# Queries by seven products, the ratio on GpSimd and rows in pairs, in a two-layer decoder trunk

## The chip, the cores and the metric

The kernel runs on one core of a Trainium2 chip. The metric is the device time in microseconds (us) of one execution; of several runs the median is taken. One more execution was recorded by the hardware profiler, and all views of the profile come from that one. The engines are called TensorE (PE in the profile, and PEld for its weight loads), VectorE (DVE), ScalarE (ACT), GpSimd (POOL) and SyncE (SP), whose queue issues most DMA transfers.

## The reference

The input `x` (512 rows of 1024) gets 16 learned meta rows ahead of it, 528 rows in all. Two layers follow, each with a norm, one input projection, a mixing step, a gate and an output projection of width 2048 to 1024; then a last norm. Layer 1 is gated linear attention and the change does not touch it. Layer 2 is differential attention with 8 heads; per head the two softmax maps are subtracted:

```python
q, k, v, z = jnp.split(xn @ w_in, 4, axis=-1)        # 2048 columns each, 256 a head
s = jnp.einsum('bhpqd,bhpkd->bhpqk', qb, kh) * scale + bias   # p = 0, 1: two maps of 128 columns
p = jax.nn.softmax(causal(s), axis=-1)
a = p[:, :, 0] - lam * p[:, :, 1]
o = head_rms(jnp.einsum('bhqk,bhkv->bhqv', a, vh)) * gnorm * (1.0 - lambda_init)
y = jax.nn.silu(z) * o
h = h + y @ w_out
```

Inputs and output are float32.

## The kernel before

**Numbers.** Every matmul operand in float32 is kept as two parts, a rounded `hi` and the rest `lo`; a product is the sum of `hi*hi`, `hi*lo` and `lo*hi`. The helper `split` (lines 276 to 280) makes the parts: ScalarE copies `hi`, VectorE subtracts to get `lo`. So each weight block that is used is passed once through ScalarE and once through VectorE.

**Two forms of a projection.** A block of 256 output columns of a projection (one head's queries, keys, values or gates) is made in one of two ways.
- *Plain* (`project`, matmul at line 421): for each 128 columns, 8 blocks of the contraction times three terms, each matmul 512 columns wide. The weights come in by `load_w` and are split as two pairs (`want_diff`).
- *A unit* (class `Unit`, `product` with the matmul at line 431): a 2 by 2 block scheme of the Strassen-Winograd kind, seven products instead of eight, each of 12 matmuls over half of the rows (256 columns without the meta rows, 264 with them). `want_unit` loads the weights and makes, on VectorE, four sums of 128x512 (line 366), and five operands: the single blocks `a11`, `a12`, `a22` and the pairs `s21` and `s43`. The products are `first` (p1) and `p2` to `p7`. p1, p6 and p7 accumulate in one PSUM bank, `self.bx`; after each of them `partial` (line 452) has ScalarE copy the bank to SBUF. `add` (lines 477 and 479) has VectorE combine another bank with such a copy. When half of the output is there, `tail` is called.

A unit knows whether the next thing in the queue is a unit too (`nxt`); then it computes that one's first product ahead of its own last two, and the next one finds itself `early`. A unit that is `early` and has no `nxt` is called lone here.

**Buffers.** PSUM has banks `bx` (two of them), `by`, `bv` (one each) for projections, and four `ps` for the attention. Weight operands have one buffer for each single block and two for pairs; raw weights have two.

**The order of the work.** TensorE's order is the order of the program text. A `Weaver` (`W`) holds a queue of generators, one a projection; `W.fill(us)` runs them for about so many microseconds by the costs that they yield, and between two fills the program issues a step of the attention. The other engines are ordered by the scheduler, by readiness and by priority (`urgent`, `at_once`, `soon` raise it). Each engine executes in its order.

**The head loop** (the loop over `hd` near the end of `trunk`). In pass `hd` the attention of head `hd` is woven with the projections for head `hd + 1`: first, in passes 2 to 6, `q_diff_out2`, an output projection of an earlier pair of heads (matmuls at line 400, and an add into `hacc` on VectorE at line 1783 for each row block); then gates `z`, values `v`, keys `k` as units and queries `q` plain. In pass 6 the order is `k`, `q`, `v`, `z`. The steps of the attention are, for each of four blocks of 128 query rows:
- `A` = `scores`: matmuls of `q` and `k` (line 400, `ps<-k,q`), for each of the two maps a VectorE instruction that adds the bias and finds the minimum (line 1692), an exponential on ScalarE with its row sum (1694); then on VectorE the reciprocal of the second map's sum (1697), the ratio `lam * sum0 / sum1` (1698), and the combination of both maps (1699).
- `B` = `turn`: transposes on TensorE, and their split.
- `C` = `values`: matmuls with `v`; ScalarE squares (1728), GpSimd takes the power -1/2 (1730), ScalarE scales (1731).
- `E` = `rows`: two transposes on TensorE (1737), a multiplication with the gate on VectorE (1740), and a split.

The first step `A(3)` of pass `hd` needs the queries that were the last projection of pass `hd - 1`. The last pass is cut short, and the rest of its steps is written out behind the loop, between the last output projections (line 1807).

## Time and profile before

| | |
|---|---|
| median of 3 runs | 971.12 us (970.82 to 972.05) |
| profiled execution | 970.65 us, of it 968.9 us from the first to the last instruction |
| ScalarE's copies of weight pairs (line 276, `wh<-raw`) | 98, 1054 ns each |
| VectorE's subtractions of weight pairs (line 277, `wl<-raw,wh`) | 98, 1221 ns each |
| ScalarE's copies of a unit's bank (line 452) | 120, 379 ns each |
| GpSimd's power in `values` (line 1730) | 32, 795 ns each |
| memory read and written | 83.64 and 11.80 MB, 99 GB/s over the span |

How to read the views: the page gives busy time and share of the span by engine, and the chain that ended last, followed back from the last instruction. A row of groups has line, engine, operation, output<-inputs, shapes and count; then busy us and mean ns of one; then the engine's idle time ahead of them and what ended most of it. A row of the timeline has the start in us, the duration in us, and the same names; in brackets the idle time before it. Matmuls overlap in the pipeline, so what one costs is read from start to start, not from its duration. A window's row gives the busy time of each engine in that stretch.

### The profile page before, as it was taken

The numbers are of one execution on the slowest core, as the hardware profiler recorded it, in microseconds if no ns is written. First come the engines' busy times: TensorE is split into PE (matmuls) and PEld (weight loads), VectorE is DVE, ScalarE is ACT, GpSimd is POOL, SyncE is SP. The second block draws the span as 40 slices with busy tenths as digits, with TensorE's granted clock in tenths as the row PEclk, the third lists the DMA queues.
The fourth block names the chain that finished last, engine by engine and source line by source line (L and its number), as shares of the span: only waits on it lengthen the run. The fifth ranks groups of instructions, "written<-read, shape, count | busy, mean of one in ns | idle before, by whom it ended". The sixth has DMA issues, their size and how long they took to land.

```text
span 968.9 us, 18048 instructions
## 1 busy us (share of the span) xinstructions
PE 957.2 (99%) x6993; PEld 906.9 (94%) x6993; DVE 778.6 (80%) x1586; ACT 626.8 (65%) x1304; POOL 44.9 (5%) x68
## 2 busy tenths in 40 slices
PE   9999999999999999999999999999999999999997
PEld 8999999999999999998899998998999989989996
DVE  7989885886888787668997987968869769687785
ACT  7776755577647567656757776575675756755583
POOL 1000000000000000000001001000000000000001
PEclk9999999999999999999999999999999999999999
DMA  7322223635363236124355525243342341722212
GB/s 197 88 85 59 82 79 122 147 103 128 116 162 91 85 117 158 53 101 152 99 130 138 143 73 133 75 139 98 99 138 88 118 119 44 182 70 84 89 64 87
DMA packets 128522, 104.94 MB, mean 108 GB/s; under 512 B 51102, under 2 KB 112830, under 8 KB 128433
## 3 DMA queue, kind: packets, MB, share of 16 engines
q1 hardware_dynamic: 123104, 93.80, 35.1%
q10 hardware_dynamic: 5328, 9.95, 2.8%
q8 instruction: 56, 0.92, 0.4%
q14 instruction: 34, 0.27, 0.1%
HBM read 83.64 MB, written 11.80 MB: 99 GB/s over the span
## 4 chain that ended last, share of the span: by engine, by line
PE 88%; ACT 1%; DVE 1%; issue 1%; POOLq 0%; DVEq 0%
PE bx L431 19%; PE bv L431 12%; PE by L431 10%; PE bx L421 10%; PE ps L400 9%; PE bx L972 5%; PE bx L400 3%; PE bv L972 2%; PE by L972 2%; PE ps L1214 2%; PE by L400 2%; PE bv L400 2%; PE ps L1807 1%; PE bx L1807 1%; PE bv L421 1%; PE by L421 1%
## 5 line engine op out<-in xcount | busy, mean ns | idle before, releaser
L277 DVE TENSOR_TENSOR wl<-raw,wh 128x1024 fp32r<-128x1024 f32 x98 | 119.4, 1221 | 23.0 <-ACT wh L276 18.9
L276 ACT ACTIVATE wh<-raw 128x1024 fp32r<-128x1024 f32 x98 | 103.1, 1054 | 48.3 <-PE by L972 22.9
L431 PE MATMUL bv<-x,wh 128*128 128x264 f32 (+1 forms) x656 | 98.6, 287 | 0.0
L431 PE MATMUL bx<-x,wh 128*128 128x264 f32 (+1 forms) x640 | 95.6, 286 | 0.0
L431 PEld LDWEIGHTS bv<-x,wh 128*128 128x128 f32 x656 | 86.8, 189 | 0.6 <-DVE z L479 0.2
L431 PEld LDWEIGHTS bx<-x,wh 128*128 128x128 f32 x640 | 84.6, 188 | 0.7 <-ACT u L452 0.2
L452 ACT ACTIVATE u<-bx 128x264 f32<-128x264 f32 (+1 forms) x120 | 45.3, 379 | 35.5 <-PE bx L431 33.1
L1694 ACT ACTIVATE p<-p,st 128x528 f32<-128x528 f32 (+3 forms) x64 | 36.5, 570 | 41.7 <-DVE st L1692 41.4
L421 PE MATMUL bx<-x,wh 128*128 128x512 f32 (+1 forms) x256 | 62.4, 385 | 0.0
L277 DVE TENSOR_TENSOR wl<-sum,wh 128x1024 fp32r<-128x1024 f32 x41 | 50.1, 1221 | 10.6 <-ACT wh L276 10.5
L431 PE MATMUL bx<-x,wl 128*128 128x264 f32 (+1 forms) x320 | 54.1, 284 | 0.0
L431 PE MATMUL bv<-x,wl 128*128 128x264 f32 (+1 forms) x328 | 53.8, 284 | 0.1
L421 PEld LDWEIGHTS bx<-x,wh 128*128 128x128 f32 x256 | 44.4, 188 | 7.8
L276 ACT ACTIVATE wh<-sum 128x1024 fp32r<-128x1024 f32 x41 | 43.1, 1051 | 9.7 <-PE by L972 3.9
L431 PE MATMUL by<-x,a12h 128*128 128x264 f32 (+1 forms) x320 | 47.5, 286 | 0.1
L1730 POOL TENSOR_TENSOR st<-st,mhalf 128x1 f32<-128x1 f32 x32 | 25.5, 795 | 468.6 <-ACT on L1728 418.2
L431 PE MATMUL bx<-x,a11h 128*128 128x264 f32 (+1 forms) x320 | 46.6, 284 | 0.0
L431 PEld LDWEIGHTS bv<-x,wl 128*128 128x128 f32 x328 | 45.4, 188 | 0.3 <-issue 0.3
L431 PEld LDWEIGHTS bx<-x,wl 128*128 128x128 f32 x320 | 45.3, 188 | 0.3
L431 PEld LDWEIGHTS bx<-x,a11h 128*128 128x128 f32 x320 | 42.4, 188 | 0.6
L431 PEld LDWEIGHTS by<-x,a12h 128*128 128x128 f32 x320 | 42.1, 188 | 0.3 <-ACT t L1658 0.3
L276 ACT ACTIVATE a11h<-raw 128x512 fp32r<-128x512 f32 x41 | 25.7, 626 | 20.7 <-DMA raw<-in_diff_w_in_dram 7.9
(493 smaller groups left out, 2631.9 us busy)
## 6 DMA issues: line engine op xcount, KB each, us to landing
raw<-in_gla_w_in_dram SPq DMA_DIRECT2D x48, 512.0 KB, 4.5
raw<-in_diff_w_in_dram SPq DMA_DIRECT2D x42, 512.0 KB, 4.9
raw<-in_diff_w_in_dram SPq DMA_DIRECT2D x11, 1024.0 KB, 5.9
raw<-in_gla_w_out_dram SPq DMA_DIRECT2D x8, 1024.0 KB, 5.8
raw<-in_diff_w_out_dram SPq DMA_DIRECT2D x8, 1024.0 KB, 6.0
vd<-planes ACTq DMA_DIRECT2D x12, 268.0 KB, 5.8
vd<-keep ACTq DMA_DIRECT2D x12, 264.0 KB, 2.3
T<-bdr SPq DMA_DIRECT2D x8, 264.0 KB, 4.7
```

The costliest lines, as they stand in the source:

```text
L276: act.activation(hi, src, AF.Copy)
L277: dve.tensor_tensor(lo, src, hi.bitcast(F32), op=ALU.subtract)
L400: pe.matmul(ps, l, r, start=first and n == 0, stop=last and n == 2, **kw)
L421: pe.matmul(bank, a[:, k, :], b[k] if n0 is None else b[k][:, n0 + i * nn:n0 + (i + 1) * nn], start=n == 0 and ks[0] == 0, stop=n == len(t ...
L431: pe.matmul(bank[:, :x[q].shape[2]], w[p][:, k * P:(k + 1) * P], x[q][:, k, :], start=first and i == 0, stop=i == len(PASSES) - 1, skip_gr ...
L452: W.moved = act.activation(t, self.bx[:, :self.n], AF.Copy, scale=self.sc)
L972: pe.matmul(banks[i][:, :HT], h.t[p][:, k, mm * P:(mm + 1) * P], s.y[q][k][:, i * HT:(i + 1) * HT], start=n == 0, stop=n == len(PASSES) - 1)
L1214: pe.matmul(o, s.kd[:, i, kc], s.qs[:, i, t0:t0 + n], start=i == 0, stop=i == 1)
L1694: act.activation(p[:, :nk], p[:, :nk], AF.Exp, scale=-1.0, bias=st[:, m:m + 1], accum_out=st[:, 2 + m:3 + m])
L1730: pool.tensor_tensor(ms, ms, mhalf[:, :1], op=ALU.pow)
L1807: pe.matmul(ps[i], yp[hd][p][:, k, b * P:(b + 1) * P], wt[q][cs.start // 512][:, 2 * hd + k, cs.start % 512:(cs.stop - 1) % 512 + 1], star ...
```

## The change

- Queries of heads 3 to 7 become units over the rows without meta; their tail splits the finished half into `s.q`.
- In layer 2 a lone unit computes p7 in a second `bx` bank of its own; VectorE adds the earlier copy to it instead of ScalarE copying the accumulated bank.
- `q_diff_out2`, behind the second part's row block 1 of its last half, issues the first product of the unit that follows it.
- In `scores` the second map is made before the first. The ratio moves from two VectorE instructions to three on GpSimd: a power of -1, and two multiplications.
- `rows` handles two blocks at once (except in the last head): four transposes, one multiplication and one split of twice the width. The loop has two `E` steps instead of four.
- The first fill of a pass is 4.0 instead of 3.0, and the least fills behind `B` and `E` are 2.4 and 1.0 instead of none.

```diff
@@ class Unit
+        @at_once
+        def third(self, bank):
+            t = T(up[0], [P, HT], F32, "u", bufs=3)[:, :self.n]
+            if self.sc == 1.0:
+                dve.tensor_tensor(t, bank[:, :self.n], self.u2, op=ALU.add)
+            else:
+                dve.scalar_tensor_tensor(t, bank[:, :self.n], self.sc, self.u2, op0=ALU.mult, op1=ALU.add)
+            return t
...
             def p7():
-                yield from product(self.bx, ws.use(s43)[1], X["t3"], False)
-                self.u3 = self.partial()
+                if W.second and early and not nxt:
+                    bank = pb_tile("bx")
+                    yield from product(bank, ws.use(s43)[1], X["t3"])
+                    self.u3 = self.third(bank)
+                else:
+                    yield from product(self.bx, ws.use(s43)[1], X["t3"], False)
+                    self.u3 = self.partial()
                 add(1, 1, self.bv, self.u3, -1)
@@ trunk
+    minus = cp.tile([P, 1], F32, name="minus")
+    dve.memset(minus, -1.0)
...
-    up[0] = ep
+    up[0], W.second = ep, True
@@ q_diff_q
+        scale, qts = -float(P) ** -0.5, []
+
+        def tiles():
+            assert not hd or heads[hd - 1].scored
+            s.q = [T(ep, [P, 2, NR], F32R, f"q{j}", bufs=1) for j in range(2)]
+
+        if hd in (3, 4, 5, 6, 7):
+            def dst():
+                tiles()
+                qts.extend([tok_tile()[:, :NR], tok_tile()[:, :NR]])
+                return qts
+
+            @soon
+            def tail(i):
+                split(*[t[:, i, :] for t in s.q], qts[i])
+
+            return W.add(Unit(want_unit(d_w_in, 256 * hd), Xr, scale, dst, tail), 8.9)
         want_diff(256 * hd)
@@ scores
-            r.p = []
+            r.p = [None, None]
...
-            for m in range(2):
+            for m in (1, 0):
...
-                r.p.append(p[:, :nk])
-
-            dve.reciprocal(st[:, 5:6], st[:, 3:4])
-            dve.scalar_tensor_tensor(st[:, 5:6], st[:, 5:6], lam, st[:, 2:3], op0=ALU.mult, op1=ALU.mult)
+                r.p[m] = p[:, :nk]
+
+            pool.tensor_tensor(st[:, 5:6], st[:, 3:4], minus, op=ALU.pow)
+            pool.tensor_tensor(st[:, 4:5], st[:, 2:3], lam, op=ALU.mult)
+            pool.tensor_tensor(st[:, 5:6], st[:, 5:6], st[:, 4:5], op=ALU.mult)
             dve.scalar_tensor_tensor(r.p[0], r.p[1], st[:, 5:6], r.p[0], op0=ALU.mult, op1=ALU.subtract)
@@ rows
-        def rows(r):
+        def rows(*rs):
+            w = P * len(rs)
             pt = ps_tile()
             for m in range(2):
-                pe.transpose(pt[:, m * P:(m + 1) * P], r.on[:, m * P:(m + 1) * P], ident)
-            y = T(ep, [P, 2, P], F32, "yt")
-            cs = slice(r.ta, r.ta + P)
-            W.mark = dve.tensor_tensor(y, pt[:, :256].rearrange("p (m c) -> p m c", m=2), s.z[:, :, cs], op=ALU.mult)
+                for j, r in enumerate(rs):
+                    pe.transpose(pt[:, m * w + j * P:m * w + (j + 1) * P], r.on[:, m * P:(m + 1) * P], ident)
+            y = T(ep, [P, 2, w], F32, "yt", bufs=1)
+            cs = slice(rs[0].ta, rs[0].ta + w)
+            W.mark = dve.tensor_tensor(y, pt[:, :2 * w].rearrange("p (m c) -> p m c", m=2), s.z[:, :, cs], op=ALU.mult)
...
-        return A, lambda b: turn(R[b]), lambda b: values(R[b]), lambda b: rows(R[b])
+        return A, lambda b: turn(R[b]), lambda b: values(R[b]), lambda b: rows(*([R[b]] if hd == D_HEADS - 1 else [R[b], R[b + 1]]))
@@ q_diff_out2
         def gen():
+            nxt = W.following()
+            nxt = nxt if isinstance(nxt, Unit) else None
...
                         yield 1.4
+                        if (i, j, b) == (halves[-1], 1, 1) and nxt:
+                            yield from nxt.first()
@@ head loop
-        steps = [(A, 0), (A, 1), (B, 0), (A, 2), (C, 0), (B, 1), (E, 0), (A, 3), (C, 1), (B, 2), (E, 1), (C, 2), (B, 3),
-                 (E, 2), (C, 3), (E, 3)]
+        steps = [(A, 0), (A, 1), (B, 0), (A, 2), (C, 0), (B, 1), (A, 3), (C, 1), (B, 2), (E, 1), (C, 2), (B, 3),
+                 (C, 3), (E, 3)]
...
-        W.fill(3.0)
+        W.fill(4.0)
...
-                       ((4.0, 3.0, 5.2, 3.0, 4.6, 3.0, 4.0, 3.0)[hd]) if n == len(steps) - 2 else 2.4 if f is C else 0.0))
+                       ((4.0, 3.0, 5.2, 3.0, 4.6, 3.0, 4.0, 3.0)[hd]) if n == len(steps) - 2 else {A: 0.0, B: 2.4, C: 2.4, E: 1.0}[f]))
```

More of the change, by code (lines that the diff above doesn't have):

```diff
@@ L78, in __init__ @@
         self.queue, self.late, self.left, self.stop = deque(), [], 0.0, None
-        self.away, self.behind, self.gated = [], [], ()
+        self.away, self.behind, self.gated, self.second = [], [], (), False
     def add(self, gen, us=0.0):
@@ L1668, in gen @@
                 yield from project(ws.take(), real2, None, NR, [by_halves(bank)])
-                assert not hd or heads[hd - 1].scored
                 if i == 0:
-                    s.q = [T(ep, [P, 2, NR], F32R, f"q{j}", bufs=1) for j in range(2)]
-                urgent(split)(*[t[:, i, :] for t in s.q], bank, scale=-float(P) ** -0.5)
+                    tiles()
+                urgent(split)(*[t[:, i, :] for t in s.q], bank, scale=scale)
         return W.add(gen(), 10.3)
```

## The prediction

> **What bounds the kernel now.** I read the page first: how full each engine is, and whose work the chain that ended last is made of.
>
> ```profile
> span 968.9 us, 18048 instructions
> PE 957.2 (99%) x6993; PEld 906.9 (94%) x6993; DVE 778.6 (80%) x1586; ACT 626.8 (65%) x1304; POOL 44.9 (5%) x68
> PE 88%; ACT 1%; DVE 1%; issue 1%; POOLq 0%; DVEq 0%
> ```
>
> TensorE is 99% busy, and 88% of the last chain is TensorE's own work. A busy TensorE can still hide waits, so I went on to the windows, one for each pass of the head loop that the change touches (a pass runs from one `A(3)` to the next), and two fuller stretches before them.
>
> ```profile
> core 0: us, PE busy (x) PEld busy (x) DVE busy (x) ACT busy (x) POOL busy (x), PEclk, DMA share, GB/s
> 460.00:520.00 60.00, 59.11 (x441) 56.44 (x441) 58.04 (x112) 39.05 (x79) 1.21 (x1) 1.00 0.44 113
> 485.00:548.00 63.00, 62.85 (x478) 60.36 (x476) 54.90 (x120) 41.42 (x98) 4.05 (x4) 1.00 0.58 141
> 667.87:730.90 63.03, 63.03 (x436) 58.70 (x434) 49.96 (x109) 41.14 (x92) 2.97 (x4) 1.00 0.35 107
> 730.90:794.00 63.10, 63.10 (x436) 58.70 (x435) 48.77 (x108) 40.87 (x92) 3.15 (x4) 1.00 0.37 107
> ...
> 915.00:969.00 54.00, 47.12 (x315) 42.89 (x313) 37.50 (x87) 31.99 (x86) 5.13 (x8) 0.97 0.19 69
> ```
>
> A pass takes 63.1 us, and in it TensorE has no idle time at all, while VectorE works 48.8 of it and ScalarE 40.9. So in these passes time is saved by fewer matmul columns, and by nothing else. An edit that only takes away a wait of TensorE finds no wait there to take away. The converse is the danger: any new wait of TensorE is lost in full. The last window has 6.9 us of idle TensorE; nothing in the change shortens its end.
>
> **The saving: queries of five heads by seven products.** The plain query projection issues 24 matmuls of 512 columns for each half of the head, 48 in all. As a unit it issues 7 products of 12 matmuls with 256 columns, 84 in all. The timeline gives the pace of both; the start of one row to the start of the next is what a group costs.
>
> ```profile
> 657.94 3.90 PE L421 MATMUL bx<-x,wh 128*128 128x512 f32 x16
> 661.68 0.63 PE L421 MATMUL bx<-x,wl 128*128 128x512 f32 x2
> ...
> 679.22 1.11 PE L431 MATMUL by<-x,a12h 128*128 128x256 f32 x8
> 680.16 0.63 PE L431 MATMUL by<-x,a12l 128*128 128x256 f32 x4
> 680.63 0.64 PE L431 MATMUL bx<-x,wh 128*128 128x256 f32 x4
> ```
>
> Sixteen matmuls of 512 columns take 661.68 - 657.94 = 3.74 us, 0.234 each; twelve of 256 columns (a gate's product) take 680.63 - 679.22 = 1.41 us, 0.1175 each. So 48 x 0.234 = 11.22 us become 84 x 0.1175 = 9.87 us: 1.35 us a head, and 6.75 us for the five heads 3 to 7, whose queries run in the passes 2 to 6. All of it lies on the engine that sets the time.
>
> **What the units cost VectorE and ScalarE.** Rows of the groups in the pass 730.9 to 794.0, VectorE's and one of ScalarE's:
>
> ```profile
> L277 DVE TENSOR_TENSOR wl<-raw,wh 128x1024 fp32r<-128x1024 f32 x7 | 8.6, 1222 | 1.0 <-ACT wh L276 1.0
> L277 DVE TENSOR_TENSOR a11l<-raw,a11h 128x512 fp32r<-128x512 f32 x3 | 2.1, 690 | 4.9 <-ACT a11h L276 4.8
> L366 DVE TENSOR_TENSOR sum<-sum,raw 128x512 f32<-128x512 f32 x3 | 2.1, 689 | 0.0
> L1740 DVE TENSOR_TENSOR yt<-ps,z 128x256 f32<-128x256 f32 x4 | 1.7, 419 | 2.0 <-PE ps L1737 2.0
> L277 DVE TENSOR_TENSOR hT<-yt,hT 128x256 fp32r<-128x256 f32 x4 | 1.7, 418 | 0.0
> L277 DVE TENSOR_TENSOR k<-t,k 128x512 fp32r<-128x512 f32 x2 | 1.4, 686 | 0.4 <-ACT k L276 0.4
> L280 DVE SCALAR_TENSOR_TENSOR q<-bx,q 128x512 fp32r<-128x512 f32 x2 | 1.4, 683 | 0.0
> L1698 DVE SCALAR_TENSOR_TENSOR st<-st,lam 128x1 f32<-128x1 f32 x4 | 0.9, 216 | 0.1
> L479 DVE TENSOR_TENSOR t<-by,u 128x256 f32<-128x256 f32 x1 | 0.4, 416 | 0.0
> L1697 DVE RECIPROCAL st<-st 128x1 f32<-128x1 f32 x4 | 0.6, 158 | 0.9 <-ACT p L1694 0.9
> ...
> L276 ACT ACTIVATE a11h<-raw 128x512 fp32r<-128x512 f32 x3 | 1.9, 623 | 1.7 <-DMA raw<-in_diff_w_in_dram 1.7
> ```
>
> Weights: both forms make two pairs of 1.22 us, but the unit also makes three single blocks (3 x 0.69) and four sums (4 x 0.69): 4.83 us more on VectorE. Taking the banks out: 2 x 0.68 go; four adds and the third product's add (5 x 0.42) and two splits from SBUF (2 x 0.69) come: 2.1 us more. Against it: the ratio leaves VectorE, 4 x (0.158 + 0.216) = 1.5 us, and the rows in pairs replace 4 x (0.419 + 0.418) by two of each at 512 columns, 4 x 0.69, 0.6 us less. The sum is 4.8 us: 48.8 becomes 53.6 us of a pass that shrinks to 61.75, or 87%. ScalarE gets 3 x 0.62 us for the single blocks and small change; it has 22 us free. What hides this work is VectorE's 14.3 us of idle time. That such a load can be carried is shown by the window 485 to 548: VectorE 54.90 of 63.00, also 87%, and TensorE 62.85. If that cover were gone, VectorE would set the time (a rival, below).
>
> **The first product inside the output projection** moves 1.41 us of TensorE's work and removes none. It adds a wait. The product needs the bank `bx` that held row block 0 of the same half, and only VectorE's add into `hacc` (line 1783) frees it. Until now there were three more blocks between, now there is block 1 and, as the fill shares work out (4.2 us of projection after `A(3)`), the scores `A(2)`. So TensorE would start it where `bv` now starts. Of the four passes 2 to 5, in order, the add on VectorE, and the start of `bv`:
>
> ```profile
> 611.14 0.68 DVE L1783 TENSOR_TENSOR keep<-keep,bx 128x512 f32<-128x512 f32 x1
> 611.63 0.39 PE L400 MATMUL bv<-wh,hT 128*128 128x512 f32 x1
> ...
> 673.98 0.68 DVE L1783 TENSOR_TENSOR keep<-keep,bx 128x512 f32<-128x512 f32 x1
> 674.53 0.39 PE L400 MATMUL bv<-wh,hT 128*128 128x512 f32 x1
> ...
> 737.37 0.68 DVE L1783 TENSOR_TENSOR keep<-keep,bx 128x512 f32<-128x512 f32 x1
> 737.61 0.39 PE L400 MATMUL bv<-wh,hT 128*128 128x512 f32 x1
> ...
> 800.71 0.39 PE L400 MATMUL bv<-wh,hT 128*128 128x512 f32 x1
> ...
> 801.92 0.68 DVE L1783 TENSOR_TENSOR keep<-keep,bx 128x512 f32<-128x512 f32 x1
> ```
>
> The add ends 0.19, 0.13, 0.44 and 1.89 us after that start. Were VectorE's order to stay, TensorE would wait 2.65 us in the four passes. The order will not stay: the units change what is queued there. Bounds: 0 (the adds come first) and 7.05 (each add also sits behind VectorE's wait for the ratio, 1.1 us, below). I take the three small waits and half of the large one, 0.76 + 0.95 = 1.7 us, as the first three passes agree and the fourth is the odd one.
>
> **The ratio on GpSimd.** Two VectorE instructions become three on GpSimd; the power overlaps the second exponential, the two multiplications come after it. They gate VectorE's combination of `p` (line 1699); behind it on VectorE are queued weights and the adds of line 1783, so TensorE's `bx` waits for it. `B`, which transposes `p`, comes some 4 us of fill or more later. How long a GpSimd instruction takes:
>
> ```profile
> 518.79 1.72 POOL L1730 TENSOR_TENSOR st<-st,mhalf 128x1 f32<-128x1 f32 x1 [66.75 <-ACT on L1728]
> ...
> 518.83 0.68 DVE L277 TENSOR_TENSOR a12l<-raw,a12h 128x512 fp32r<-128x512 f32 x1
> ...
> 782.16 0.55 POOL L1730 TENSOR_TENSOR st<-st,mhalf 128x1 f32<-128x1 f32 x1 [6.75 <-ACT on L1728]
> ```
>
> 0.55 us alone (782.16), 1.72 while VectorE ran weights (518.79). Where VectorE itself waits, the short value holds: 2 x 0.55 = 1.1 us after the exponential against 0.37 before. Four times a pass that is up to 4.4 us of VectorE's idle time, and nothing where the order puts weights into the gap. Both fit into 61.75 - 53.6 = 8.1 us. It costs the time nothing by itself; its part at the bank is in the bound above.
>
> **The rest at nothing.** The third product of lone units in a bank of its own takes away TensorE's wait for ScalarE's copy of the bank; the windows have no such wait, and the 0.42 us on VectorE is counted. Rows in pairs leave the eight transposes as they are. `m` in the order 1, 0 matches the unit, whose half 0 is ready last: it gives that half another six matmuls of slack. The first fill of 4.0 instead of 3.0 still means three blocks of 1.4 us in passes 2 to 6. Weight bytes are the same, in two transfers instead of one.
>
> **Sum.** The profiled execution took 970.65 us (span 968.9). 970.65 - 6.75 + 1.7 = 965.6. The median of the runs is 971.12, 0.47 above the profiled one, so 966.1 for the median.
>
> **Rivals.** *The bank and the ratio eat the gain.* The adds of line 1783 come behind the waiting combination: 2.65 + 4 x 1.1 = 7.05 us of new waits against 6.75: 970.95, as a median 971.4. For it: VectorE already waits in order at that place (0.9 us before line 1697). Against: weights can be put into the gap. I give it 0.20, spread from 968.5 to 971.4.
>
> *VectorE sets the time: slower.* The place is the passes 2 to 6, the price its 53.6 us plus all idle time that it cannot shift. It decides from 8.1 us of such idle time a pass. If the waits of the rows above stay (4.8 for `a11h`'s transfer, 2.0 for the rows' transposes) and the ratio adds 4.4, that is 64.8 us a pass against 63.1: 5 x 1.7 = 8.5 us more, 979.6. Against: a VectorE that is behind does not wait for what has long arrived; from 460 to 520 it worked 58.04 of 60.00, and TensorE still 59.11. 0.08.
>
> *GpSimd holds VectorE up: slower too.* If a VectorE instruction with two SBUF operands had to wait for a running GpSimd instruction, 12 of them a pass at 0.55 us would make 53.6 + 6.6 = 60.2, with the ratio's 4.4 us 64.6: 5 x 1.5 us above the pass of now, 978.6. The trace speaks against it: `a12l` started 0.04 us into the GpSimd instruction and took its usual 0.68 us; GpSimd was the one stretched, to 1.72. 0.03. The Trainium skill (SBUF — State Buffer, "Who interferes with whom") says that a VectorE instruction with two SBUF inputs contends with a GpSimd instruction that reads SBUF, and that the one that starts first blocks the other; by it this rival would be the likelier. The rows here agree that the two collide, and differ on who yields.
>
> **How the numbers follow.** My forecast, with bank waits from 0 to 3.7 us (964.4 to 968.1), has 0.69; the rivals 0.20, 0.08, 0.03. Under 0.2% (1.9 us) a measurement of this kernel can't tell from no change: from 969.2 to 973.1 is "same". The first rival lies there with 0.12 of its 0.20. Faster: 0.69 + 0.08 = 0.77; same 0.12; slower 0.08 + 0.03 = 0.11. The range goes from the forecast without any bank wait, less the 0.3 that the lowest run lies under the median, 964.1, to 970.8 inside the first rival; the slower cases and the first rival's end stay out.
>
> **What would show it.** Right: passes of about 61.75 us from 606 to 857, TensorE full but for 0.1 to 1 us ahead of the first product in the projection; VectorE near 87% there; line 421 gone from passes 2 to 6; GpSimd at 0.55 us and more, twelve ratio instructions a pass. The first rival would show as waits of line 431's `bx` for line 1783 above 1 us in each pass, with line 1699 waiting for GpSimd just ahead of that add. VectorE as the bound would show as TensorE waits spread over a whole pass with VectorE above 95%. I am wrong about the saving if 84 matmuls of 256 columns do not keep 0.1175 us.

## The result and the profile after

The kernel after takes 978.14 us (median of 6 runs, 976.12 to 981.35), the kernel before 971.34 us beside it (6 runs, 970.82 to 972.05): a ratio of 1.0072, interval 1.006 to 1.0084. It is slower, where 966.1 was forecast. The profiled execution took 976.12 us (span 974.3), the lowest of the six. The slowest run, of 981.35, had the lowest mean granted clock, 0.991 against 0.995 to 0.999 in the others.

From the page of the kernel after, the span, the busy time of the engines, the chain's shares, and one group of matmuls:

```profile
span 974.3 us, 18491 instructions
PE 954.1 (98%) x7173; PEld 912.4 (94%) x7173; DVE 799.3 (82%) x1557; ACT 636.1 (65%) x1313; POOL 84.3 (9%) x164
PE 77%; DVE 6%; ACT 4%; DMA 2%; issue 1%; POOL 1%; SPq 0%; POOLq 0%; DVEq 0%; ACTq 0%
L431 PE MATMUL bx<-x,a11h 128*128 128x264 f32 (+1 forms) x360 | 53.6, 286 | 6.8 <-DVE keep L1820 6.8
```

TensorE's own work fell from 88% to 77% of the last chain, and 6% of it is VectorE now. One line of matmuls waited 6.8 us, for VectorE's add into `hacc` (line 1820 here, 1783 before). The windows, one for each of the passes 2 to 6:

```profile
core 0: us, PE busy (x) PEld busy (x) DVE busy (x) ACT busy (x) POOL busy (x), PEclk, DMA share, GB/s
605.95:668.32 62.37, 62.05 (x472) 59.69 (x471) 52.16 (x104) 41.13 (x94) 8.16 (x16) 1.00 0.35 101
668.32:731.85 63.53, 62.08 (x472) 59.62 (x471) 56.46 (x114) 43.26 (x96) 8.04 (x16) 1.00 0.35 107
731.85:796.21 64.36, 62.68 (x471) 59.80 (x470) 54.05 (x108) 42.38 (x95) 7.95 (x16) 1.00 0.37 105
796.21:860.97 64.76, 62.10 (x472) 59.72 (x470) 53.93 (x108) 42.43 (x95) 7.71 (x16) 1.00 0.37 107
860.97:918.25 57.28, 56.51 (x394) 52.22 (x392) 49.64 (x98) 35.04 (x83) 6.88 (x16) 1.00 0.24 76
```

TensorE is busy 62.1 to 62.7 us of the passes 2 to 5, less than the 62.9 to 63.1 of before. But it idles 0.3, 1.5, 1.7 and 2.7 us in them, where it idled not at all. VectorE is at 83 to 89%, near the 87% of the forecast, and not full. The waits of the kernel after that are new, with total, count and longest:

```profile
DVE p L1732 <- POOL st L1731: 18.3, 28, 1.4
...
PE bx L431 <- DVE keep L1820: 6.8, 5, 2.7
...
PE ps L400 <- DVE vm L412: 1.1, 1, 1.1
```

VectorE waits 28 times for GpSimd's last multiplication, and TensorE 5 times for VectorE's add: the 0.3, 1.5, 1.7 and 2.7 us of the passes 2 to 5, and 0.7 in pass 6. The last row is one wait in pass 7, of the scores' matmuls for another VectorE instruction. The timeline of the dearest wait for the add, in pass 5:

```profile
801.72 1.22 DVE L277 TENSOR_TENSOR wl<-sum,wh 128x1024 fp32r<-128x1024 f32 x1
801.79 1.26 PE L400 MATMUL ps<-k,q 128*128 128x400 f32 x6
801.83 1.16 POOL L1730 TENSOR_TENSOR st<-st,lam 128x1 f32<-128x1 f32 x1 [1.12 <-ACT p L1726]
803.06 0.20 POOL L1731 TENSOR_TENSOR st<-st 128x1 f32<-128x1 f32 x1
803.29 0.77 DVE L1732 SCALAR_TENSOR_TENSOR p<-p,st,p 128x528 f32<-128x528 f32 x1 [0.36 <-POOL st L1731]
803.98 0.56 DVE L1724 CUSTOM_DVE_ANT_0 p<-ps,T 128x400 f32<-128x400 f32 x1
...
804.47 0.57 DVE L1724 CUSTOM_DVE_ANT_0 p<-ps,T 128x400 f32<-128x400 f32 x1
...
804.97 0.68 DVE L1820 TENSOR_TENSOR keep<-keep,bx 128x512 f32<-128x512 f32 x1
...
805.70 0.74 PE L431 MATMUL bx<-x,a11h 128*128 128x256 f32 x4 [2.66 <-DVE keep L1820]
```

Read upwards from the end: TensorE waits 2.66 us for the add at 804.97; ahead of the add in VectorE's order stand both `A` instructions of the next block (803.98, 804.47), ahead of those the combination (803.29), and that waited 0.36 us for GpSimd. The first multiplication there took 1.16 us, as long as VectorE's subtraction beside it. In the passes 2 to 4 the combination stands ahead of the add too, and it waits 0.36 or 0.37 us for GpSimd. What comes between differs: nothing in pass 2, a subtraction of weights (1.22 us) in pass 3, the two `A` instructions in pass 4. In pass 6 no combination is there; VectorE had waited 1.90 us for ScalarE's copy of weights.

**Where 10.5 us went** (976.12 against the 965.6 forecast for the profiled execution). Pass 2 starts at 605.95, 1.0 us later than before. Passes 2 to 5 take 255.0 us against 252.1: 3.0 more, where 3.7 less were forecast (four heads x 1.35, less 1.7), so 6.7. Of these, 4.4 are waits for the add (6.1 against 1.7); the other 2.3 lie in TensorE's busy time, and their cause is open. From pass 6 on it is 113.3 against 111.9: 1.5 more, where 1.35 less was forecast, so 2.8; 0.7 of it is the fifth wait for the add and 1.1 the wait in pass 7.

### The profile page after: what moved, and what is told of

Its sections match the earlier page's. It is cut to its first block, busy times and chain, and to the rows that moved or that the text cites. A ratio compares the mean times of both kernels' runs of the same rounds, so it can differ in the third digit from the quotient of the medians.

```text
span 974.3 us, 18491 instructions
## 1 busy us (share of the span) xinstructions
PE 954.1 (98%) x7173; PEld 912.4 (94%) x7173; DVE 799.3 (82%) x1557; ACT 636.1 (65%) x1313; POOL 84.3 (9%) x164
## 4 chain that ended last, share of the span: by engine, by line
PE 77%; DVE 6%; ACT 4%; DMA 2%; issue 1%; POOL 1%; SPq 0%; POOLq 0%; DVEq 0%; ACTq 0%
PE bx L431 20%; PE bv L431 12%; PE by L431 11%; PE ps L400 8%; PE bx L988 5%; PE bx L421 3%; PE by L988 2%; PE bv L988 2%; PE ps L1230 2%; PE bx L400 2%; DMA raw<-in_diff_w_in_dram 2%; PE bv L400 1%; DVE wl L277 1%; ACT wh L276 1%; PE ps L1846 1%
## 5 line engine op out<-in xcount | busy, mean ns | idle before, releaser
L431 PE MATMUL bv<-x,wh 128*128 128x264 f32 (+1 forms) x736 | 108.9, 285 | 0.0
L431 PE MATMUL bx<-x,wh 128*128 128x264 f32 (+1 forms) x720 | 105.6, 285 | 0.0
L431 PEld LDWEIGHTS bv<-x,wh 128*128 128x128 f32 x736 | 96.8, 188 | 0.7 <-DVE z L488 0.2
L431 PEld LDWEIGHTS bx<-x,wh 128*128 128x128 f32 x720 | 94.4, 188 | 0.7 <-ACT ps L1760 0.2
L277 DVE TENSOR_TENSOR wl<-sum,wh 128x1024 fp32r<-128x1024 f32 x46 | 56.2, 1221 | 11.3 <-ACT wh L276 11.0
L431 PE MATMUL bv<-x,wl 128*128 128x264 f32 (+1 forms) x368 | 62.2, 286 | 0.1
L431 PE MATMUL bx<-x,a11h 128*128 128x264 f32 (+1 forms) x360 | 53.6, 286 | 6.8 <-DVE keep L1820 6.8
L1729 POOL TENSOR_TENSOR st<-st,minus 128x1 f32<-128x1 f32 x32 | 21.5, 670 | 282.8 <-ACT p L1726 282.8
L556 POOL TENSOR_TENSOR st<-st,mhalf 128x1 f32<-128x1 f32 (+1 forms) x20 | 12.1, 606 | 386.1 <-DVE st L555 386.1
L431 PE MATMUL by<-x,a22h 128*128 128x264 f32 (+1 forms) x280 | 40.1, 284 | 0.0
```

The lines of the kernel that those rows point to most:

```text
L277: dve.tensor_tensor(lo, src, hi.bitcast(F32), op=ALU.subtract)
L431: pe.matmul(bank[:, :x[q].shape[2]], w[p][:, k * P:(k + 1) * P], x[q][:, k, :], start=first and i == 0, stop=i == len(PASSES) - 1, skip_gr ...
L556: pool.tensor_tensor(dst, dst, mhalf[:np_, :dst.shape[1]], op=ALU.pow)
L1729: pool.tensor_tensor(st[:, 5:6], st[:, 3:4], minus, op=ALU.pow)
```

## The experiments

Three theories. **Bank**: the early first product waits for its bank, behind VectorE's add. **Ratio**: VectorE's waits in order for GpSimd delay what stands behind them, the add and other things. **Load**: the units' extra work makes VectorE late everywhere. The results, each with the kernel before on the same chip (970.75 to 970.93 us there, 971.34 in the comparison above); the kernels are the kernel after or before with the edit named:

| run | edit | median us (range) | ratio to before |
|---|---|---|---|
| e1 | after, first product not early | 973.95 (972.93 to 974.84) | 1.0028 [1.0017, 1.0039] |
| e2 | after, ratio on VectorE | 971.37 (969.81 to 973.5) | 1.0004 [0.9995, 1.0014] |
| e5 | after, both of these | 971.6 (969.69 to 973.6) | 1.0005 [0.9995, 1.0015] |
| e3 | before + units | 971.05 (970.45 to 972.23) | 1.0003 [0.9993, 1.0013] |
| e8 | e3 without the units' weight sums | 969.19 (967.98 to 969.92) | 0.998 [0.9971, 0.999] |
| e4 | before + early first product | 972.65 (972.05 to 973.97) | 1.0019 [1.001, 1.0029] |
| e7 | before + ratio on GpSimd | 975.25 (974.89 to 976.23) | 1.0042 [1.0025, 1.0059] |
| e9 | e7, combination issued later | 975.01 (974.08 to 975.76) | 1.004 [1.0026, 1.0054] |
| e13 | before + only the power on GpSimd | 971.05 (970.55 to 971.9) | 1.0003 [0.9994, 1.0012] |
| e14 | before + maps in the order 1, 0 | 972.14 (970.54 to 975.13) | 1.0012 [1.0003, 1.0021] |
| e17 | after, only the power on GpSimd | 970.86 (969.96 to 971.39) | 0.9999 [0.999, 1.0008] |
| e10 | after, first product one block later | 972.5 (971.63 to 974.7) | 1.0017 [1.0008, 1.0026] |
| e6 | e2, first product one block later | 968.52 (967.02 to 969.48) | 0.997 [0.996, 0.998] |
| e11 | e6 without the third product's bank | 967.05 (966.88 to 967.5) | 0.996 [0.9946, 0.9973] |
| e12 | e6 without pairs and longer fills | 970.16 (968.38 to 972.19) | 0.9993 [0.9984, 1.0002] |
| e15 | e11 with plain queries | 973.45 (972.99 to 976.4) | 1.0034 [1.0021, 1.0048] |
| e16 | e11, first fill 3.0 | 967.55 (967.04 to 968.19) | 0.9967 [0.9955, 0.9979] |
| e18 | e11, power on GpSimd | 966.92 (966.58 to 968.31) | 0.9965 [0.9951, 0.9979] |

### The ratio on GpSimd

**e2**, on the kernel after:

```diff
-            pool.tensor_tensor(st[:, 5:6], st[:, 3:4], minus, op=ALU.pow)
-            pool.tensor_tensor(st[:, 4:5], st[:, 2:3], lam, op=ALU.mult)
-            pool.tensor_tensor(st[:, 5:6], st[:, 5:6], st[:, 4:5], op=ALU.mult)
+            dve.reciprocal(st[:, 5:6], st[:, 3:4])
+            dve.scalar_tensor_tensor(st[:, 5:6], st[:, 5:6], lam, st[:, 2:3], op0=ALU.mult, op1=ALU.mult)
```

> The changed kernel with the ratio back on VectorE as a reciprocal and a product. Ratio theory: the waits of the bank shrink to the 2.65 us that the order of before gave, 972 us. Bank theory: the add stays behind the weights, the waits change by less than 1.5 us in sum, 975 to 977 us. Load theory: 1.5 us more of VectorE's work a pass, later adds, 977 to 979 us.

971.37 us: undoing this one edit gives 6.8 of the 978.14 back. What is left of the bank wait, from the waits of e2:

```profile
PE bx L431 <- DVE keep L1819: 2.3, 2, 1.7
```

These are 1.7 us in pass 3 and 0.6 in pass 6. So 4.5 of the 6.8 us of bank waits went with the ratio. **e7** puts the ratio alone into the kernel before, with the maps in the order 1, 0:

```diff
...
-            dve.reciprocal(st[:, 5:6], st[:, 3:4])
-            dve.scalar_tensor_tensor(st[:, 5:6], st[:, 5:6], lam, st[:, 2:3], op0=ALU.mult, op1=ALU.mult)
+            pool.tensor_tensor(st[:, 5:6], st[:, 3:4], minus, op=ALU.pow)
+            pool.tensor_tensor(st[:, 4:5], st[:, 2:3], lam, op=ALU.mult)
+            pool.tensor_tensor(st[:, 5:6], st[:, 5:6], st[:, 4:5], op=ALU.mult)
```

> The kernel before with nothing but the ratio on GpSimd and the maps in the order 1, 0. Bank theory: three row blocks lie between the add and the next use of the bank, so nothing waits, 970.5 to 971.5 us. Ratio theory (VectorE's order with the wait for GpSimd delays whatever comes behind it): 972 to 974 us. Load theory: 1.5 us less of VectorE's work a pass, 970.5 to 971 us.

975.25 us, 4.3 us for an edit that touches no TensorE instruction, in a kernel without an early first product, and more than the ratio theory's 972 to 974. Its waits, and its timeline in pass 4:

```profile
DVE p L1702 <- POOL st L1701: 23.2, 30, 2.3
...
PE bx L431 <- ACT u L452: 3.4, 4, 1.4
```

```profile
748.37 0.43 DVE L1694 CUSTOM_DVE_ANT_0 p<-ps,T 128x272 f32<-128x272 f32 x1
...
748.90 0.52 ACT L1696 ACTIVATE p<-p,st 128x272 f32<-128x272 f32 x1 [3.30 <-DVE st L1694]
...
749.42 0.36 ACT L452 ACTIVATE u<-bx 128x256 f32<-128x256 f32 x1
...
749.84 1.21 PE L431 MATMUL bx<-x,wh 128*128 128x256 f32 x8 [1.30 <-ACT u L452]
```

This is the second road of the delay. VectorE is late with the minimum of `A` (748.37); ScalarE, in its order, waits 3.30 us for it with an exponential; behind that stands the copy of a unit's bank (749.42), and TensorE, which wants the bank back, waits 1.30 us. ScalarE's order is another one, too. The same copy and exponential in the kernel before:

```profile
746.09 0.39 ACT L452 ACTIVATE u<-bx 128x256 f32<-128x256 f32 x1 [2.00 <-PE bx L431]
746.94 0.52 ACT L1694 ACTIVATE p<-p,st 128x272 f32<-128x272 f32 x1 [0.46 <-DVE st L1692]
```

There the copy comes first. Counted from the start of the pass (730.90 before, 731.94 in e7), the minimum (746.40 before) is 0.9 us later in e7 and the copy 2.3 us.

**e9** is e7 with the combination issued behind 2.5 us of fill, at the latest ahead of `turn`:

```diff
-            dve.scalar_tensor_tensor(r.p[0], r.p[1], st[:, 5:6], r.p[0], op0=ALU.mult, op1=ALU.subtract)
+            r.mix = urgent(lambda: dve.scalar_tensor_tensor(r.p[0], r.p[1], st[:, 5:6], r.p[0], op0=ALU.mult, op1=ALU.subtract))
...
+            W.defer(2.5, mix)
```

> The kernel before with the ratio on GpSimd (975.25 us alone), and the combination of the two maps issued some 2.5 us of projection work after the ratio instead of right behind it, so that VectorE need not stand waiting for GpSimd. Ratio theory (the 4.3 us are VectorE's in-order waits for GpSimd at the combination, handed on to ScalarE's exponentials and copies and so to TensorE): VectorE's 23 us of waits at the combination fall below 5 us and the time returns to 971 to 972 us. Rival (the 4.3 us come from the new order of the two maps, or from GpSimd's instructions getting in the way of others, wherever the combination stands): 974 to 975.5 us.

It stayed at 975.01, the rival's figure. But the waits of e9 show that the edit did not do what it was meant to:

```profile
DVE p L1702 <- POOL st L1701: 22.3, 29, 2.3
```

VectorE waits for GpSimd as long as in e7. The scheduler orders VectorE by readiness and priority, and moving the place in the program text did not move the instruction: ahead of the first combination of pass 4 it waits 1.44 us in both. So e9 tells the two theories apart in nothing. **e13** takes the wait away in another manner: with the maps in the order 1, 0, only the power, which needs the first exponential alone, is on GpSimd.

```diff
...
-            dve.reciprocal(st[:, 5:6], st[:, 3:4])
+            pool.tensor_tensor(st[:, 5:6], st[:, 3:4], minus, op=ALU.pow)
             dve.scalar_tensor_tensor(st[:, 5:6], st[:, 5:6], lam, st[:, 2:3], op0=ALU.mult, op1=ALU.mult)
```

> The kernel before with the maps in the order 1, 0 and only the power of -1 on GpSimd, where it runs during the second exponential; the ratio itself stays one VectorE instruction behind that exponential, as in the kernel before. Ratio theory (the 4.3 us of the ratio on GpSimd are the two multiplications that VectorE must wait for after the second exponential): 970.5 to 971.8 us, VectorE waiting for GpSimd less than 3 us in all. Rival (any instruction of GpSimd in the chain costs, or the order of the maps does): 973 to 975 us.

971.05 us, no cost. The waits of e13 for GpSimd:

```profile
DVE st L1700 <- POOL st L1699: 2.0, 4, 0.7
```

23.2 us of waits became 2.0, and the 4.3 us went with them, though GpSimd still does an instruction of 0.63 us on average for each ratio. **e14** changes the order of the maps alone:

```diff
-            for m in range(2):
+            for m in (1, 0):
```

> The kernel before with nothing but the maps in the order 1, 0. Ratio theory: 970.5 to 971.5 us, no difference. Rival (the order of the maps, and not GpSimd, is what the ratio on GpSimd alone paid 4.3 us for): 974 to 975 us.

972.14 us, nearer to no difference than to 974; its interval leaves out 1 by a little. Its profiled execution is the longest run, 975.13, and passes 2 to 5 in it are as before (62.9 to 63.1 us); the difference lies in pass 7, where the granted clock is 0.5 from 942 to 944 us, behind two waits of 1 us each. As e13 has the same order of the maps and no cost, the order does not explain e7. **e17** is the e13 edit inside the whole change:

> The kernel after (978.14 us) with only the power of -1 left on GpSimd; the ratio itself is again one VectorE instruction behind the second exponential. Ratio theory, now that the power alone cost nothing in the kernel before: all of the 6.8 us that the ratio on GpSimd cost in the change comes back: 970.5 to 972 us, bank waits of line 431 near 2 us. Rival (in the fuller order of the change the power on GpSimd is stretched by VectorE's work and is late too): 974 to 977 us, VectorE waiting for the power.

970.86 us: all that the ratio cost comes back although the power stays on GpSimd. So the price comes with the two multiplications behind the second exponential. The timeline of VectorE in e17, at the place in pass 5 that is shown above:

```profile
799.31 1.22 DVE L277 TENSOR_TENSOR wl<-sum,wh 128x1024 fp32r<-128x1024 f32 x1
800.44 0.22 DVE L1730 SCALAR_TENSOR_TENSOR st<-st,lam 128x1 f32<-128x1 f32 x1
800.58 0.68 DVE L1819 TENSOR_TENSOR keep<-keep,bx 128x512 f32<-128x512 f32 x1
801.17 0.77 DVE L1731 SCALAR_TENSOR_TENSOR p<-p,st,p 128x528 f32<-128x528 f32 x1
801.85 0.57 DVE L1724 CUSTOM_DVE_ANT_0 p<-ps,T 128x400 f32<-128x400 f32 x1
```

The ratio follows the subtraction at once, and the add comes right behind it, 1.27 us after the subtraction's start; in the kernel after the add started 3.25 us after it (801.72, 804.97). So the delay is part wait and part order: with GpSimd in the chain the add was placed behind the combination and the next block's `A`. No run here takes the wait away and keeps the order, so how much each of them costs stays open.

### The early first product

**e1** leaves out the early call, on the kernel after; **e4** adds it alone to the kernel before:

```diff
-            nxt = W.following()
-            nxt = nxt if isinstance(nxt, Unit) else None
...
-                        if (i, j, b) == (halves[-1], 1, 1) and nxt:
-                            yield from nxt.first()
```

> The changed kernel, but the output projection no longer issues the first product of the unit behind it. Bank theory (the early first product waits for VectorE's add of row block 0, 6.7 us in passes 2 to 5, and nothing else is lost by it): those waits go, nothing takes their place, about 976.1 - 6.7 = 969.4 us. Load theory (VectorE is late by the units' extra 4.8 us a pass, and the bank is only where that shows): the gates' own start or another bank waits instead, 973 to 976 us. Ratio theory (VectorE's wait for GpSimd ahead of the add is what makes it late): as the bank theory here, 969 to 970 us.

973.95 us: 4.2 us back, and not the 6.8 of the bank waits, since others came; it is the load theory's figure. From the waits of e1:

```profile
PE bx L431 <- ACT u L452: 3.0, 4, 1.1
```

This is e7's road, ScalarE's copy, with the ratio still on GpSimd.

> The kernel before with nothing but the first product of the gates inside the output projection. Bank theory: the adds of before end 0.19, 0.13, 0.44 and 1.89 us behind the place where the product would start, so 2 to 4 us of waits at the bank: 973 to 975 us. Load theory: without the units VectorE is not late, under 1 us of waits, 971 to 972 us. Ratio theory: 2.65 us of waits, 973.8 us.

972.65 us, 1.8 more than the kernel before. The profile of e4 has one wait for line 1785's add, of 1.2 us in pass 5, the place where the prediction saw 1.89 us; the three small ones that it saw did not come. **e5** undoes both the early product and the ratio's move:

> The changed kernel without the early first product and with the ratio on VectorE; units, third product, rows in pairs and fills stay. Bank theory (now: the early product and the ratio's order make the loss together, and the rest is sound): the bank's waits are gone, 967 to 969 us. Load theory (the units fill VectorE, and what they save is lost wherever VectorE is next late): 970 to 972 us, like the units alone at 971.05 us.

971.6 us, no better than e2, and again the load theory's figure. So with the ratio on VectorE the early product was worth nothing at block 1. And as e1 differs from e5 in the ratio alone, the ratio costs 2.4 us in this kernel. **e6** (on e2) and **e10** (on the kernel after) place it one block later:

```diff
-                        if (i, j, b) == (halves[-1], 1, 1) and nxt:
+                        if (i, j, b) == (halves[-1], 1, 2) and nxt:
```

> The changed kernel with the ratio on VectorE and the early first product one row block later, behind block 2. Bank theory: 1.4 us more room for the add, so the 2.3 us of waits that were left at the bank with the ratio on VectorE go, 971.4 - 2.3 = 969 us. Load theory: the waits move to other places, 970.5 to 972 us.

> The kernel after, ratio still on GpSimd, but the early first product comes behind row block 2 of the projection instead of block 1. Bank theory (the ratio costs the change 6.8 us because the add that frees the bank is pushed behind it): with one block more of slack the bank waits of 6.8 us go and the time falls to 969 to 970 us, near the 968.5 us of the same kernel with the ratio on VectorE. Ratio theory (VectorE's waits for GpSimd reach TensorE by ScalarE's copies of the units' banks as well): 972 to 974 us, the bank waits gone and waits for the copy of line 452 in their place.

e6 takes 968.52 us, 2.9 under e2, 3.1 under e5 and 2.4 under the kernel before; its bank wait is 0.4 us. e10 takes 972.5: the later place gives back 5.6 us of the kernel after, and the ratio on GpSimd still costs 4.0 (972.5 against 968.52), near the 4.3 of e7. The time is the ratio theory's, not the bank theory's 969 to 970, but the sign that the ratio theory named is missing: the profile of e10 has 1.3 us of bank waits left and no wait of 0.2 us or more for the copy of line 452. Which waits make up the 4.0 is open.

### The units and the rest

**e3** adds only the change's `q_diff_q` to the kernel before; **e8** leaves out the four weight sums of these units (VectorE's 4 x 0.69 us a head), so its queries are other ones:

```diff
+            if not sums_too:
+                return None
...
-            add(block(raw, 0), block(raw, 1), in_rows(su.t[:, 0, :]))
+            if sums_too:
+                add(block(raw, 0), block(raw, 1), in_rows(su.t[:, 0, :]))
...
```

> The kernel before with nothing but the queries of heads 3 to 7 as units. Bank theory: the columns' 6.1 us show nearly in full, 965 to 967 us. Load theory: VectorE at 55 to 56 us of a 61.8 us pass makes TensorE wait, 969 to 974 us. Ratio theory: as the bank theory.

> The kernel before with the queries of heads 3 to 7 as units whose four weight sums are left out (those five units multiply unsummed blocks), which takes 2.8 us a pass off VectorE. TensorE's work is that of the units alone (971.05 us). Load theory: VectorE is no longer late, at least half of the 6.1 us that the columns save shows: 966 to 968 us. Rival, latency: the units' queries are ready later than plain ones whatever VectorE's load, and the next head's scores wait: 970 to 971 us.

e3 gains nothing (971.05). By its waits, a unit's product waits 0.8 us for ScalarE's copy of the bank and an attention step 0.8 us for the rows; the rest is scattered over many small ones. e8 is 1.9 us faster than e3, between what the load theory (966 to 968) and its rival (970 to 971) said: VectorE's work explains a part. Whether the saving is there at all was asked of the fastest version, **e15**, which is e11 with all queries plain:

```diff
-        if hd in (3, 4, 5, 6, 7):
+        if hd in ():
```

> The fastest version (ratio on VectorE, first product behind row block 2, no bank of its own for the third product; 967.05 us) with the queries of all heads plain again. If the units' saving of 6.1 us of TensorE's work arrives in full here, where the new waits are gone: 972.5 to 973.5 us. Load theory (half of it is lost to VectorE's longer work even here): 970 to 971 us. If the units bring nothing, as they did alone: 966.5 to 967.5 us.

973.45 us against 967.05: 6.4 us for five heads. The windows of e11, passes 2 to 5, and then that of e15, pass 5:

```profile
605.63:667.72 62.09, 62.09 (x471) 59.82 (x470) 53.41 (x114) 42.32 (x96) 3.09 (x4) 1.00 0.35 103
667.72:729.83 62.11, 62.11 (x472) 59.66 (x471) 55.53 (x117) 43.71 (x97) 2.79 (x4) 1.00 0.36 109
729.83:791.69 61.86, 61.86 (x471) 59.69 (x470) 54.92 (x115) 42.95 (x96) 3.20 (x4) 1.00 0.39 110
791.69:853.51 61.82, 61.82 (x472) 59.73 (x470) 53.62 (x115) 42.83 (x96) 3.04 (x4) 1.00 0.39 112
```

```profile
795.45:858.51 63.06, 63.06 (x435) 58.73 (x434) 48.15 (x102) 38.86 (x87) 3.44 (x4) 1.00 0.39 113
```

TensorE is full in all of them. Pass 5 takes 61.82 us with units and 63.06 with plain queries: 1.24 a head, 6.2 for five. VectorE carries 53.4 to 55.5 us in the passes of e11, and TensorE shows no idle time there.

**e11**, **e12**, **e16** and **e18** look at the small edits, each from e6 or e11:

```diff
-    up[0], W.second = ep, True
+    up[0] = ep
```

> The fastest version so far (ratio on VectorE, first product behind row block 2; 968.5 us) without the third product's own bank: a lone unit accumulates it as the kernel before does. The prediction put this edit at nothing: 968.0 to 969.0 us. If the own bank takes away a wait of TensorE for ScalarE's copy that the units' load has opened: 970 to 971 us, with new waits of line 431's bx for the copy of line 452. Load theory (VectorE is rid of 0.42 us a pass): 967.5 to 968.3 us.

967.05 us, 1.5 under e6 and under all that was expected. The intervals of the two overlap, so that the third product's own bank costs something is likely and not settled.

e12, on e6, takes back the rows in pairs, the two `E` steps and the fills:

```diff
-        W.fill(4.0)
+        W.fill(3.0)
...
-        return A, lambda b: turn(R[b]), lambda b: values(R[b]), lambda b: rows(*([R[b]] if hd == D_HEADS - 1 else [R[b], R[b + 1]]))
+        return A, lambda b: turn(R[b]), lambda b: values(R[b]), lambda b: rows(R[b])
```

> The fastest version so far (968.5 us) with the rows one block at a time, in four steps, and the fills of the kernel before. The prediction put these edits at nothing: 968.0 to 969.5 us. If rows in pairs are what lets VectorE carry the units (0.6 us less work a pass and half as many stops for TensorE's transposes): 970 to 971.5 us. If the longer wait for both blocks and the longer fills cost something: 966 to 967.5 us.

970.16 us. In its profiled execution the passes 2, 3 and 5 are as full as e11's; pass 4 has one wait of 1.9 us (for `t` of line 486) and about half the clock behind it. It is 1.6 us slower than e6, and the intervals of the two do not overlap: the pairs, their two steps and the fills together are worth something here. How much is open, as the one wait and its clock alone make up more than the 1.6 in that execution.

e16 has only the first of e12's two edits that are shown, e18 has e13's edit, both on e11:

> The fastest version (967.05 us) with the first fill of a pass at 3.0 instead of 4.0. The prediction put this at nothing, as it still means three blocks of 1.4 us in passes 2 to 6: 966.5 to 967.5 us. If the first fill matters in the passes without an output projection (0, 1 and 7 lose 1.3, 0.1 and 1.9 us in this version): down to 965.5 us or up to 968.5 us.

> The fastest version (967.05 us) with the power of -1 on GpSimd in place of VectorE's reciprocal, the ratio behind it still on VectorE. VectorE is rid of 4 x 0.158 = 0.6 us a pass and is near 88% busy: 966.5 to 967.5 us by the ratio theory, since TensorE waits for little that VectorE could bring earlier. Rival (the power is late where VectorE is fullest): 968 to 970 us.

967.55 and 966.92 us: neither can be told from e11's 967.05, so the first fill is not what e12 lost. These are the fastest kernels here, 3.8 us or 0.4% under the kernel before.

## Why the prediction was wrong

- **The saving** was right: 1.35 us a head forecast, 1.24 measured where nothing hides it (e11, e15).
- **The failed step is the ratio on GpSimd**: "Both fit into 61.75 - 53.6 = 8.1 us. It costs the time nothing by itself; its part at the bank is in the bound above." It costs 4.3 us alone (e7) and 6.8 in the change (e2), and nothing once the two multiplications are one VectorE instruction again (e13, e17). The bound of 1.1 us for one wait was even too large: 18.3 us of waits over 32 ratios are 0.57 each, and a multiplication takes 0.20 us by itself where 0.55 was taken. Wrong was to set them against VectorE's idle time in a sum. Each wait, and the order that was made around it, shifts what stands behind it on VectorE, and two of these things have TensorE at their end: the add that frees the bank, and the minimum that ScalarE's exponential, and so its copies, wait for. The prediction looked only at the first. The waits of the kernel after show the first; e7 and e1 show the second.
- **The bank wait** was mis-sized: 1.7 us taken for four passes, 6.1 measured in them, and 0.7 in pass 6, which the prediction did not count. With the ratio on VectorE it is 2.3 (e2) or 2.7 (e17) in all. That this is near the 2.65 of the unshifted order is luck: the large wait, 1.7 or 1.8 us, is in pass 3, where the prediction saw 0.13, and pass 5, where it saw 1.89, has none or 0.4. The first rival had the mechanism, a waiting combination ahead of the add, and all four passes show it. But that wait is 0.36 us and not 1.1, and the rest is what else stands between; so it is luck, too, that 6.1 is near its 7.05. Its time, 971.4, set the whole saving of the units against these waits.
- **A second step failed**: "What hides this work is VectorE's 14.3 us of idle time." VectorE's load itself was forecast well, 53.6 us a pass against 52.2 to 56.5 measured. But the units alone gain nothing (e3), and the change without the ratio on GpSimd is still at 971.37 (e2), 5.3 above the forecast, of which the larger bank wait explains 0.6. The saving shows in e11, behind the later first product (3.1 us, e6 against e5) and without the third product's bank. e8 shows that VectorE's work is a part of what hid it; the rest is open. The total of idle time does not say when an instruction is due.
- **The rivals on the other side** did not come about. Their times, 979.6 and 978.6, lie near the measured 978.14 by luck. VectorE was never above 89% in these passes; and of the waits that the first of the two added up, the 4.8 us put down to the transfer for `a11h` were waits for ScalarE's copy. GpSimd did not hold VectorE up by running: in e13 and e17 it runs its power for each ratio, and the time is that of before. The row at 518.79 did not show that, though, as the last section says.
- **The rest at nothing**: the third product's bank may have cost up to 1.5 us (e6 against e11); the fill of 4.0 shows no effect (e16); the pairs, their steps and the fills together gained something (e12). Open are the 1.0 us ahead of pass 2 and some 1 us of the 2.8 from pass 6 on.

## What to carry to other kernels

Idle time of an engine can hide more work, but not a wait in its order: for each new wait, list what stands behind it on that engine and on the next ones, and ask which of these TensorE needs, and when. Work may go to a slow engine where it overlaps something that is waited for anyway (the power beside the second exponential), not at the end of the chain. A step moved earlier needs the slack of what frees its buffer: behind block 1 the early product was worth nothing (e2 against e5), one row block later 3.1 us (e6 against e5).

## What the runs showed of the hardware

**GpSimd's small instructions stretch beside VectorE.** A multiplication of 128x1 took 0.20 us by itself (803.06) and 1.16 us when it started 0.11 us into VectorE's subtraction of two SBUF operands (801.72); it ended 0.05 us after it, and the subtraction took its usual 1.22 us. The Trainium skill (SBUF — State Buffer, "Who interferes with whom") says that such a pair contends and that the one that starts first blocks the other. This row agrees. The prediction took the row at 518.79 of the kernel before, where GpSimd's power took 1.72 us, for one that differs, as GpSimd had started 0.04 us ahead of `a12l`. But another VectorE instruction with both operands in SBUF was running then, until 518.91:

```profile
518.42 0.49 DVE L1699 SCALAR_TENSOR_TENSOR p<-p,st,p 128x272 f32<-128x272 f32 x1
```

So VectorE was first there too, and the row agrees. Where GpSimd did start with no such instruction under way, at 815.13 of the kernel before, its power took its 0.55 us, and VectorE's sum of 128x512, begun 0.08 us behind it, its usual 0.68: there neither was held up, so blocking by GpSimd is not seen.

**Half the clock after short waits, at times.** The windows of e12 around its wait of 1.9 us, which ended at 769.37, and then those of the kernel after around the wait of 2.66 us that ended at 805.70 (the clock is the third column from the end):

```profile
768.00:770.00 2.00, 0.63 (x5) 0.63 (x6) 1.97 (x6) 0.11 (x1) 0.00 (x0) 1.00 0.00 0
770.00:772.00 2.00, 2.00 (x13) 2.00 (x13) 2.00 (x4) 1.83 (x4) 0.00 (x0) 0.62 0.00 1
772.00:774.00 2.00, 2.00 (x12) 2.00 (x12) 1.08 (x4) 1.75 (x4) 0.00 (x0) 0.53 0.86 270
774.00:776.00 2.00, 2.00 (x19) 2.00 (x18) 0.47 (x2) 1.49 (x4) 0.00 (x0) 1.00 1.03 331
```

```profile
804.00:806.00 2.00, 0.30 (x2) 0.30 (x3) 2.00 (x7) 1.33 (x4) 0.55 (x2) 1.00 0.00 0
806.00:808.00 2.00, 2.00 (x16) 1.87 (x15) 1.75 (x4) 0.90 (x2) 0.38 (x2) 1.00 0.00 0
```

In e12 the wait was followed by almost 4 us at about half the clock, which costs 2 x 0.38 + 2 x 0.47 = 1.7 us more, nearly the wait again. In the kernel after a longer wait was followed by the full clock. So a wait can cost TensorE twice, and not each time. The Trainium skill (TensorE: Matmul & The Clock Gate, "Part 1: The HAM clock gate") gives an idle window of about 3.4 us as what halves the clock; in e12 a gap of 1.9 us was enough, with TensorE busy for 4 us ahead of it, so the trace does not agree that it takes so long. That the spread of the kernel after (976.12 to 981.35 us) comes from such stretches is suggested by its clocks and was not shown.
